# The last stage of a gated short-convolution layer: product f of its output matmul as seven smaller products

## The chip, the cores and the metric

The kernel runs on one core of a Trainium2 chip. Five engines work side by side, each through its own list of instructions in order: TensorE (PE, with its weight loads as PEld), VectorE (DVE), ScalarE (ACT), GpSimd (POOL) and SyncE (SP). SP and POOL also issue transfers (DMAs); POOL alone issues those that add to what stands at their destination. The metric is the device time of one execution in microseconds (us); before the change it is 767.92, the median of 3 runs (767.84 to 767.94).

## The reference

One layer, 1024 frames of 1024 channels, inner width 2048, all float32:

```python
u = rms_norm(x, pre_norm)                      # over the 1024 channels of a frame
z, bg, cg, v = split(u @ w_in, 4)              # w_in: 1024 x 8192
y = bg * causal_dwconv(cg * v, conv_w) * silu(z)   # 3 taps over frames, per channel
m = y @ w_out                                  # w_out: 2048 x 1024
out = x + rms_norm(m, post_norm)
```

The change concerns `m = y @ w_out` alone, and the sign with which some channels of `y` are kept.

## The kernel before, in words

**Arithmetic.** Float32 operands are split into two parts: `hi`, rounded by an ACT copy, and `lo`, the rest, by a DVE subtraction (`split_unit`). Each matmul of 128 channels x 128 frames x 512 columns is then three instructions (lo x hi, hi x lo, hi x hi; lines 929 to 931 in the last stage), with a weight load each.

**First stage** (to 607 us of the profile). `u @ w_in` in groups of three column blocks, 20 products a group (`product`, `read`), in an order written out by hand (`ORDER`). Tables say at which product of a group DVE, ACT, POOL and SP get which side work. The gated result `y` goes to memory: `y_d` holds it, `s_d` sums of its quarters, `t_d` sums of quarters of `w_out`. The sums are made by adding DMAs from POOL (`more`), each waiting for the one before where it reads its result.

**Last stage.** `y` (1024 frames x 2048 channels) and `w_out` are halved in both directions, and seven products instead of eight give the four quarters of `m`: a, b, c, e, d, f, g, in this order, each of 512 frames x 1024 channels x 512 columns. A product is 4 row tiles of 128 frames (`q`), 8 chunks of 128 channels in two halves (`h`) of four, 3 instructions each: 96 matmuls of 512 columns. a, c, d and g accumulate in the banks `po_x`, b in `po_b`, e and f in `po_v`. DVE and ACT fold them into `C11`, `C12` and `C22` (the tile `res`): `C12` holds, when f is added, all that output rows 0 to 511 need in their second half, so each of the row tiles 0 to 3 can be finished then (`norm_square` on ACT, `finish_o` on DVE, ACT and POOL, stores and the next `load_res` on SP). Rows 512 to 1023 are finished as g ends, tile by tile.

**Order around the change.** There is no scheduler: each engine's list follows the program text. The loop at the end issues for each half of a product its 48 matmuls, then four `split_unit` (operands of the product half two places later, each an ACT copy and a DVE subtraction of 128 x 1024) with two `fetch_unit` (SP transfers into the staging tiles `raw`, 6 buffers, and `u`, 18 buffers), then, after the second half, the four `combine`. For f the finishing of row tile q-1 follows the combine of tile q. g's loop runs by row tile, and within it by half: g's second half is first needed 12 matmuls after g begins.

**Signs.** `cw`, the taps of the convolution, is stored negated for channels 1024 to 2047, so that `y` of these is negative and all differences of the scheme become sums; `split_unit` turns c's operand of `w_out` back (`nc.scalar.mul(hi, src, -1.0)`).

Of the kernel before, what the change touches and what calls it, by code (L numbers as in the profile page):

```python
# [20 lines left out]
def kernel(  # L21
# [392 lines left out]


# [283 lines left out]
    nc.scalar.copy(half_of(cw, 0), half_of(pc[:, : TAPS * NC], 0))  # L699
    nc.scalar.mul(half_of(cw, 1), half_of(pc[:, : TAPS * NC], 1), -1.0)  # L700
# [111 lines left out]
    OUT = [(i, h) for i in "abcedfg" for h in (0, 1)]  # L812
    UNITS_O = [(side, i, h) for i, h in OUT for side in "uy"]
    CQ = CH // 2
    fetched, OP = [], {}

    def fetch_unit():
        n = len(fetched)
        if n >= len(UNITS_O):
            return  # L820
        side, i, h = UNITS_O[n]
        js = slice(h * CQ, (h + 1) * CQ)
        far = slice(CH + h * CQ, CH + (h + 1) * CQ)
        if side == "u":
            plain_u = {"a": wov[:, js, :HB], "b": wov[:, far, :HB], "f": wov[:, far, HB:]}
            src = plain_u[i] if i in plain_u else t_d[:, TK[i], js]
            r = []
            for q in (0, 1):
                r.append(raw.tile([P, 2, HB], F32, tag="raw", name=f"r{side}_{i}{h}{q}"))
                nc.sync.dma_start(r[q], src[:, 2 * q : 2 * q + 2])  # L830
        else:
            plain_y = {"a": y_d[:, js, :HB], "b": y_d[:, far, :HB], "g": y_d[:, far, HB:]}
            src = plain_y[i] if i in plain_y else s_d[:, SK[i], js]
            t = up.tile([P, 2, 2, HB], F32, tag="u", name=f"r{side}_{i}{h}")
            nc.sync.dma_start(t.rearrange("p a b c -> p (a b) c"), src)
            r = [t[:, 0], t[:, 1]]
        fetched.append(r)

    def split_unit(delayed=False):
        n = len(OP)  # L840
        if n >= 2 * len(UNITS_O):
            return
        side, i, h = UNITS_O[n // 2]
        q = n % 2
        t = new_u(f"o{side}_{i}{h}{q}")
        src, hi, lo = flat(fetched[n // 2][q]), flat(t[:, 0]), flat(t[:, 1])
        if (side, i) == ("u", "c"):
            nc.scalar.mul(hi, src, -1.0)
            nc.vector.scalar_tensor_tensor(lo, src, -1.0, hi.bitcast(F32), op0=ALU.mult, op1=ALU.subtract)
# [70 lines left out]
    def out_mm(i, h, q):  # L920
        which = i if i == "b" else "v" if i in "ef" else "x"
        if (which, q) not in ob:
            ob[which, q] = bank(f"po_{which}{q}")
        ps = ob[which, q]
        for k in range(CQ):
            u, y = OP["u", i, h, k // 2], OP["y", i, h, k // 2]
            hi, lo = (y[:, z, k % 2, q * P : (q + 1) * P] for z in (0, 1))
            first, last = i in "abe" and h == 0 and k == 0, h == 1 and k == CQ - 1
            nc.tensor.matmul(ps, lo, u[:, 0, k % 2], start=first, stop=False, skip_group_check=True)  # L929
# [1 line left out]
            nc.tensor.matmul(ps, hi, u[:, 0, k % 2], start=False, stop=last, skip_group_check=True)  # L931

# [60 lines left out]
    def combine(i, q):  # L993
# [8 lines left out]
        elif i == "e":  # L1002
            nc.scalar.copy(C22[:, q], v_)
        elif i == "d":
            nc.vector.tensor_add(C22[:, q], x_, C22[:, q])
            early_half(q + TH)
        elif i == "f":
            nc.vector.tensor_add(C12[:, q], v_, C12[:, q])  # L1008
            norm_square(q, 1)
# [57 lines left out]
```

## Time and profile before

| What | Value |
|---|---|
| median of the runs (lowest, highest) | 767.92 us (767.84, 767.94) |
| span of the profiled execution (first to last instruction) | 766.2 us; no other time of that execution is given |
| PE busy | 758.0 us, 99% |
| DVE, ACT, POOL busy | 485.9, 452.5, 459.7 us |
| product f, PE | 715.81 to 737.57 us |
| product g, PE | 737.57 to 759.3 us |
| mean DMA rate over the span | 152 GB/s |

The page lists busy time by engine, the chain of work that ended last (followed back from the last instruction), and groups of instructions as line, engine, operation, output<-inputs, with mean duration and what ended the idle time before them. Timeline rows begin with start and length in us. An `x2` behind a row means that two were merged. The page's busy time of PE counts pipelined matmuls that overlap; the distance between starts tells the pace. An idle engine costs nothing unless PE waits for it.

### The profile page before, as it was taken

Reading aid. Unit: us, or ns where it says so; the run is one execution under the profiler, and the core shown is the slowest. Engines: PE = TensorE matmul, PEld = TensorE weight load, DVE = VectorE, ACT = ScalarE, POOL = GpSimd, SP = SyncE. Lnnn points to the kernel's source line nnn. Section 1 sums busy time; section 2 is a strip of 40 time slices with the busy share of each in tenths; the row PEclk is TensorE's granted clock in tenths of the full one; section 3 lists DMA queues with packets and bytes.
Section 4 is the critical chain, followed back from the end, with each engine's and each line's share of the span. In section 5 each row is a group of like instructions: output and inputs, shape, how many; then the busy total and the mean of one; then the engine's idle time right before and its main releaser. Section 6 shows DMA issues by size and latency. Waiting matters only on the chain.

```text
span 766.2 us, 10006 instructions
## 1 busy us (share of the span) xinstructions
PE 758.0 (99%) x3386; PEld 627.4 (82%) x3386; DVE 485.9 (63%) x748; ACT 452.5 (59%) x881; POOL 459.7 (60%) x564
## 2 busy tenths in 40 slices
PE   9999999999999999999999999999999999999996
PEld 8888888888888888888888888888888888888885
DVE  5898776475656566656565664655566957545755
ACT  8869766557646665754666665666467735544531
POOL 0687979669676876976797796797765220000021
PEclk9999999999999999999999999999999999999999
DMA  9401335447356358165465556574545689754237
GB/s 327 142 1 64 102 97 155 133 110 191 86 154 152 94 116 213 40 183 122 134 153 128 122 151 152 124 182 98 132 97 168 205 281 373 277 189 173 79 123 261
DMA packets 103363, 116.55 MB, mean 152 GB/s; under 512 B 4696, under 2 KB 70544, under 8 KB 102288
## 3 DMA queue, kind: packets, MB, share of 16 engines
q1 hardware_dynamic: 94080, 99.13, 39.4%
q0 software_dynamic: 9216, 16.78, 14.0%
q8 instruction: 26, 0.43, 0.2%
q14 instruction: 25, 0.20, 0.1%
q10 hardware_dynamic: 16, 0.00, 0.0%
HBM read 97.02 MB, written 44.04 MB: 184 GB/s over the span
## 4 chain that ended last, share of the span: by engine, by line
PE 98%; DMA 0%; DVE 0%; ACT 0%; issue 0%; DVEq 0%
PE pX L132 8%; PE pX L134 8%; PE pX L133 8%; PE pY L132 7%; PE pY L134 7%; PE pY L133 7%; PE po_x L931 4%; PE po_x L930 4%; PE po_x L929 4%; PE pV L134 4%; PE pV L132 4%; PE pV L133 4%; PE pZ L134 2%; PE pW L134 2%; PE pW L132 2%; PE pZ L132 2%
## 5 line engine op out<-in xcount | busy, mean ns | idle before, releaser
L362 DVE TENSOR_TENSOR sn<-sn,pY 128x512 f32<-128x512 f32 x57 | 39.2, 687 | 56.4 <-PE pY L134 28.9
L969 POOL TENSOR_TENSOR res<-xr,res 128x512 f32<-128x512 f32 x4 | 6.9, 1736 | 105.4 <-DVE res L968 104.0
L338 POOL TENSOR_TENSOR g<-g,sn 128x512 f32<-128x512 f32 x29 | 40.1, 1390 | 42.2 <-ACT sn L336 35.4
L362 DVE TENSOR_TENSOR sn<-sn,pX 128x512 f32<-128x512 f32 x57 | 39.2, 688 | 33.5 <-PE pX L134 33.5
L311 POOL TENSOR_TENSOR g<-sn,g 128x512 f32<-128x512 f32 x23 | 29.9, 1298 | 47.5 <-DVE sn L360 47.5
L336 ACT ACTIVATE sn<-sn 128x512 f32<-128x512 f32 x24 | 15.2, 632 | 64.1 <-DVE sn L362 40.0
L356 ACT ACTIVATE sn<-pV 128x512 f32<-128x512 f32 x38 | 20.6, 596 | 48.0 <-PE pV L134 48.0
L320 POOL TENSOR_TENSOR g<-g,sn 128x512 f32<-128x512 f32 x20 | 28.2, 1411 | 19.2 <-DVE sn L362 18.9
L354 ACT COPY sn<-pZ 128x512 f32<-128x512 f32 x19 | 11.2, 588 | 46.6 <-PE pZ L134 46.6
L368 POOL DMA_DIRECT2D s_d<-s_d x24 | 19.8, 823 | 21.6 <-DMA s_d<-y_d 14.1
L178 POOL TENSOR_TENSOR raw<-raw 128x256 f32<-128x256 f32 x40 | 32.3, 918 | 0.0
L360 DVE TENSOR_TENSOR g<-pY,g 128x512 f32<-128x512 f32 x15 | 10.4, 692 | 30.7 <-PE pY L134 30.7
L183 POOL TENSOR_TENSOR raw<-e,raw 128x256 f32<-128x256 f32 x40 | 28.7, 739 | 1.6
L179 POOL TENSOR_TENSOR e<-raw,raw 128x512 f32<-128x512 f32 x20 | 26.2, 1312 | 1.6
L938 ACT ACTIVATE jk<-res 128x512 bf16<-128x512 f32 x12 | 7.6, 631 | 31.7 <-DVE res L1008 13.0
L132 PE MATMUL pp<-b,wn 128*128 128x512 f32 x62 | 24.6, 397 | 0.0
L133 PE MATMUL pp<-b,wn 128*128 128x512 f32 x62 | 24.3, 393 | 0.0
L134 PE MATMUL pp<-b,wn 128*128 128x512 f32 x62 | 24.2, 390 | 0.0
L301 DVE SCALAR_TENSOR_TENSOR g<-g,cw,cv 128x512 f32<-128x512 f32 x30 | 22.5, 749 | 1.7
L233 DVE TENSOR_TENSOR wE<-wE,wE 128x512 fp32r<-128x512 f32 x20 | 13.7, 686 | 14.1 <-ACT wE L232 14.0
L301 DVE SCALAR_TENSOR_TENSOR cv<-g,cw,cv 128x512 f32<-128x512 f32 x30 | 22.4, 747 | 0.0
L233 DVE TENSOR_TENSOR wC<-wC,wC 128x512 fp32r<-128x512 f32 x20 | 13.7, 687 | 11.9 <-ACT wC L228 11.9
(388 smaller groups left out, 2903.3 us busy)
## 6 DMA issues: line engine op xcount, KB each, us to landing
raw<-in_sc_w_in SPq DMA_DIRECT2D x64, 512.0 KB, 4.2
t_d<-in_sc_w_out SPq DMA_DIRECT2D x32, 256.0 KB, 4.6
s_d<-g SPq DMA_DIRECT2D x29, 256.0 KB, 2.1
s_d<-s_d POOLq DMA_DIRECT2D x24, 256.0 KB, 4.4
y_d<-g SPq DMA_DIRECT2D x23, 256.0 KB, 2.5
t_d<-in_sc_w_out POOLq DMA_DIRECT2D x16, 256.0 KB, 7.8
t_d<-t_d POOLq DMA_DIRECT2D x16, 256.0 KB, 4.8
xr<-in_x SPq DMA_DIRECT2D x8, 512.0 KB, 5.7
```

What stands on the lines that cost most here:

```text
L132: nc.tensor.matmul(ps, lo, u[:, 0, kk], start=first, stop=False, skip_group_check=True)
L133: nc.tensor.matmul(ps, hi, u[:, 1, kk], start=False, stop=False, skip_group_check=True)
L134: nc.tensor.matmul(ps, hi, u[:, 0, kk], start=False, stop=last, skip_group_check=True)
L178: 0: lambda: (add(w2[:, 0], w2[:, 0], w2[:, 1]), add(w2[:, 2], w2[:, 1], w2[:, 2])),
L183: 5: lambda: (sub(w0[:, 2], e[:, 3], w0[:, 2]), sub(w0[:, 0], e[:, 3], w0[:, 0])),
L301: nc.vector.scalar_tensor_tensor(g if j == TAPS - 1 else ps, g, tap(c, j), ps, op0=ALU.mult, op1=ALU.add)
L311: nc.gpsimd.tensor_mul(g, src, g)
L338: when([(c, "cv", h), (c, "silu", h)], (c, "z", h), {"cv": 1, "silu": 1}, lambda: nc.gpsimd.tensor_mul(cv_of(c, h), cv_of(c, h), t))
L362: nc.vector.tensor_sub(a, a, ps)
L929: nc.tensor.matmul(ps, lo, u[:, 0, k % 2], start=first, stop=False, skip_group_check=True)
L930: nc.tensor.matmul(ps, hi, u[:, 1, k % 2], start=False, stop=False, skip_group_check=True)
L931: nc.tensor.matmul(ps, hi, u[:, 0, k % 2], start=False, stop=last, skip_group_check=True)
```

## The change

Product f (`s_d["f"]` times the last quarter of `w_out`) is itself done by seven products of halved size: 256 frames (2 row tiles) x 512 channels (4 chunks) x 256 columns. They are called pieces 1 to 7 and run in the order 1, 2, 6, 5, 7, 3, 4. Each is 24 matmuls of 256 columns. What else it takes:

- Sums of quarters of f's operands, in the new memory tiles `tf_d` (from `w_out`; four plain transfers by SP at the beginning of the last group of the first stage but one, four adding ones by POOL later in it) and `sf_d` (from `s_d["f"]`; four plain and four adding ones, all by POOL, placed behind the halves of c and e).
- A small sum or difference into `C12` after each piece, on 128 x 2 x 256 numbers, by DVE. Pieces 1, 6, 7 and 4 accumulate in one bank, 5 and 3 in another, 2 has a third; a later piece of a bank waits until the earlier sum has been read from it.
- `po_v` now ends with e, which is added to `C12` too (four more DVE sums in d's time).
- Operands of a piece are two splits instead of four; both are fetched into `raw`. `refill` replaces the fixed calls of `fetch_unit`.
- Row tiles 0 and 1 are finished after piece 3, tiles 2 and 3 after piece 4.
- Negated channels are now 512 to 1535; `split_unit` turns back by product and half.

```diff
+    CQ = CH // 2
+    sf_d = dram.tile([P, 4, CQ, FC], F32, tag="sf_d", name="sf_d")
+    tf_d = dram.tile([P, 4, CQ, FC], F32, tag="tf_d", name="tf_d")
...
+    def quarter(a, i, j, k0=0, n0=0):
+        return a[:, k0 + i * CQ : k0 + (i + 1) * CQ, n0 + j * FC : n0 + (j + 1) * FC]
+    def w22(i, j):
+        return quarter(wov, i, j, CH, HB)
+    def yf(i, j):
+        return quarter(s_d[:, SK["f"]], j, i)
+    def small_t(step):
+        if step == 0:
+            for n, src in enumerate((w22(0, 0), w22(0, 0), w22(1, 1), w22(1, 0))):
+                nc.sync.dma_start(tf_d[:, n], src)
+        elif step == 1:
+            more(tf_d[:, 0], w22(0, 1))
+            more(tf_d[:, 2], w22(0, 1))
+        elif step == 2:
+            more(tf_d[:, 1], tf_d[:, 2])
+        else:
+            more(tf_d[:, 3], tf_d[:, 1])
+    def small_s(step):
+        if step == 0:
+            for n, src in enumerate((yf(1, 0), yf(0, 0), yf(1, 0), yf(0, 1))):
+                nc.gpsimd.dma_start(sf_d[:, n], src)
+        elif step == 1:
+            more(sf_d[:, 0], yf(1, 1))
+            more(sf_d[:, 2], yf(0, 0))
+        elif step == 2:
+            more(sf_d[:, 1], sf_d[:, 0])
+        else:
+            more(sf_d[:, 3], sf_d[:, 1])
...
-    nc.scalar.copy(half_of(cw, 0), half_of(pc[:, : TAPS * NC], 0))
-    nc.scalar.mul(half_of(cw, 1), half_of(pc[:, : TAPS * NC], 1), -1.0)
+    nc.scalar.copy(cw, pc[:, : TAPS * NC])
+    nc.scalar.mul(turned_chunks(cw), turned_chunks(pc[:, : TAPS * NC]), -1.0)
...
-    OUT = [(i, h) for i in "abcedfg" for h in (0, 1)]
+    FP = (1, 2, 6, 5, 7, 3, 4)
+    OUT = [(i, h) for i in "abced" for h in (0, 1)] + [("f", p) for p in FP] + [("g", 0), ("g", 1)]
...
+        if i == "f":
+            t = raw.tile([P, CQ, FC], F32, tag="raw", name=f"r{side}_f{h}")
+            nc.sync.dma_start(t, small_of(side, h))
...
+    def refill():
+        while FETCH and len(fetched) + (1 if FETCH[0][1] == "f" else 2) <= len(OP) + AHEAD:
+            fetch_unit()
...
-        if (side, i) == ("u", "c"):
+        turn = h == 6 if i == "f" else (i == "c") != (h == 1)
+        if side == "u" and turn:
...
+            if t == END - 1 and s in (2, 15, 18, 20):
+                small_t((2, 15, 18, 20).index(s))
...
+    def small_mm(p):
+        which = {1: 1, 6: 1, 7: 1, 4: 1, 2: 2, 5: 3, 3: 3}[p]
+        ...
+        for q in (0, 1):
+            o = ps[:, q * FC : (q + 1) * FC]
+            for k in range(CQ):
+                hi, lo = (y[:, z, k, q * P : (q + 1) * P] for z in (0, 1))
+                nc.tensor.matmul(o, lo, u[:, 0, k], start=p in (1, 2, 5) and q == 0 and k == 0, stop=False, skip_group_check=True)
+                nc.tensor.matmul(o, hi, u[:, 1, k], start=False, stop=False, skip_group_check=True)
+                nc.tensor.matmul(o, hi, u[:, 0, k], start=False, stop=k == CQ - 1, skip_group_check=True)
+        ps = ps.rearrange("p (a b) -> p a b", a=2)
+        for rows, cols, sign in {1: ((0, 0, 1),), 2: ((0, 0, -1),), 6: ((0, 1, -1),), 5: ((1, 1, 1),), 7: ((1, 1, 1),), 3: ((0, 1, -1),), 4: ((1, 0, -1),)}[p]:
+            c = C12[:, 2 * rows : 2 * rows + 2, cols * FC : (cols + 1) * FC]
+            if sign > 0:
+                nc.vector.tensor_add(c, ps, c)
+            else:
+                nc.vector.tensor_sub(c, c, ps)
...
         elif i == "e":
             nc.scalar.copy(C22[:, q], v_)
+            nc.vector.tensor_add(C12[:, q], v_, C12[:, q])
...
-        elif i == "f":
-            nc.vector.tensor_add(C12[:, q], v_, C12[:, q])
-            norm_square(q, 1)
...
+        if i == "f":
+            small_mm(h)
...
-        for z in range(4):
+        for z in range(2 if i == "f" else 4):
             split_unit()
-            if z % 2:
-                fetch_unit()
-        if h == 1:
+            refill()
+        if (i, h) in SMALL_S:
+            small_s(SMALL_S[i, h])
+        if i != "f" and h == 1:
             for q in range(TH):
                 combine(i, q)
-                if i == "f" and q > 0:
-                    finish_row(q - 1)
-    finish_row(TH - 1)
+        if i == "f" and h in (3, 4):
+            for q in (0, 1) if h == 3 else (2, 3):
+                norm_square(q, 1)
+                finish_row(q)
```

What this does to the order of instructions is shown at three places.

DVE before, around the end of f: the splits of g's second half (`ou_g1`, `oy_g1`), then f's first two sums (line 1008) and the finishing of row tile 0 (lines 93 to 988).

```order
L129 TENSOR_TENSOR ou_g10_6586<-ru_g10_6526,ou_g10_6586 128x1024
L129 TENSOR_TENSOR ou_g11_6589<-ru_g11_6528,ou_g11_6589 128x1024
L129 TENSOR_TENSOR oy_g10_6592<-ry_g1_6536,oy_g10_6592 128x1024
L129 TENSOR_TENSOR oy_g11_6595<-ry_g1_6536,oy_g11_6595 128x1024
L1008 TENSOR_TENSOR res_5750<-po_v0_6182,res_5750 128x512
L1008 TENSOR_TENSOR res_5750<-po_v1_6195,res_5750 128x512
L93 TENSOR_SCALAR ve_post0_6604<-so_5752,so_all_5753 128x1
L94 RECIPROCAL r0_post0_6605<-sd_post0_6602 128x1
```

DVE in the changed kernel, the same place: sum of piece 3, the first two splits of g's second half, and the beginning of row tile 0; then, after the rest of tile 0, tile 1, whose end is shown with what follows it, the sum of piece 4 and the last two splits of g.

```order
L1013 TENSOR_TENSOR res_5760<-res_5760,pf_3_6605 128x2x256
L903 SCALAR_TENSOR_TENSOR ou_g10_6699<-ru_g10_6637,ou_g10_6699 128x1024
L903 SCALAR_TENSOR_TENSOR ou_g11_6702<-ru_g11_6639,ou_g11_6702 128x1024
L96 TENSOR_SCALAR ve_post0_6708<-so_5762,so_all_5763 128x1
L97 RECIPROCAL r0_post0_6709<-sd_post0_6706 128x1
```

```order
L1050 SCALAR_TENSOR_TENSOR res_5760<-res_5760,rs_post1_6731,gpost_5756 128x512
L1070 SCALAR_TENSOR_TENSOR res_5760<-res_5760,rs_post1_6731,xr_5758 128x512
L1013 TENSOR_TENSOR res_5760<-res_5760,pf_1_6500 128x2x256
L906 TENSOR_TENSOR oy_g10_6768<-ry_g1_6672,oy_g10_6768 128x1024
L906 TENSOR_TENSOR oy_g11_6771<-ry_g1_6672,oy_g11_6771 128x1024
L96 TENSOR_SCALAR ve_post2_6777<-so_5762,so_all_5763 128x1
```

Before, the splits of g stood ahead of every sum of f and every finished row; now seven sums and the finishing of two row tiles (seven instructions each) stand ahead of the last two.

PE in the changed kernel, where d ends and piece 1 begins:

```order
L987 MATMUL po_x3_5803<-ou_d11_6322,oy_d11_6332 128x512
L988 MATMUL po_x3_5803<-ou_d11_6322,oy_d11_6332 128x512
L989 MATMUL po_x3_5803<-ou_d11_6322,oy_d11_6332 128x512
L1004 MATMUL pf_1_6500<-ou_f10_6394,oy_f10_6399 128x256
L1005 MATMUL pf_1_6500<-ou_f10_6394,oy_f10_6399 128x256
L1006 MATMUL pf_1_6500<-ou_f10_6394,oy_f10_6399 128x256
```

In all 168 instructions of 256 columns stand where 96 of 512 columns stood.

POOL in the changed kernel, from the last group but one of the first stage into the last (lines 193 to 196 make sums of `w_in` blocks, 341, 323 and 314 gate `y`, 371 issues an adding transfer):

```order
L371 DMA tf_d_80<-in_sc_w_out 128x4x256 x2
L341 TENSOR_TENSOR g_14_1_5038<-g_14_1_5038,sn_14_0_1_5375 128x512
L193 TENSOR_TENSOR e_19_5257<-e_19_5257,raw_15_3_5172 128x256
L194 TENSOR_TENSOR raw_15_3_5172<-raw_15_3_5172 128x256
L341 TENSOR_TENSOR g_14_0_5063<-g_14_0_5063,sn_14_0_0_5253 128x512
L195 TENSOR_TENSOR e_19_5257<-e_19_5257,raw_15_1_5170 128x256
L371 DMA tf_d_80<-tf_d_80 128x1024
L196 TENSOR_TENSOR raw_15_1_5170<-raw_15_1_5170 128x256
L371 DMA s_d_77<-s_d_77 128x512
L371 DMA tf_d_80<-tf_d_80 128x1024
L323 TENSOR_TENSOR g_14_0_5063<-g_14_0_5063,sn_14_1_0_5251 128x512
L314 TENSOR_TENSOR g_15_0_5314<-sn_15_3_0_5552,g_15_0_5314 128x512
```

The four transfers into `tf_d` are new in this list; the second and the third row with `tf_d` read what the one before has written.

More of the change, by code (lines that the diff above doesn't have):

```diff
@@ L810, in first_chunk, with small_of @@
             gate_y(0, 1, plain_ps[3, 1], 1, True)
-    OUT = [(i, h) for i in "abcedfg" for h in (0, 1)]
-    UNITS_O = [(side, i, h) for i, h in OUT for side in "uy"]
-    CQ = CH // 2
-    fetched, OP = [], {}
+    FP = (1, 2, 6, 5, 7, 3, 4)
+    OUT = [(i, h) for i in "abced" for h in (0, 1)] + [("f", p) for p in FP] + [("g", 0), ("g", 1)]
+    PIECES, FETCH = [], []
+    for i, h in OUT:
+        for side in "uy":
+            FETCH.append((side, i, h))
+            PIECES += [(side, i, h, q) for q in ((0,) if i == "f" else (0, 1))]
+    fetched, OP = [], {}
+    AHEAD = 4
+    def small_of(side, p):
+        if p in (5, 6, 7):
+            return (tf_d if side == "u" else sf_d)[:, p - 5]
+        if side == "u":
+            return tf_d[:, 3] if p == 4 else w22(*{1: (0, 0), 2: (1, 0), 3: (1, 1)}[p])
+        return sf_d[:, 3] if p == 3 else yf(*{1: (0, 0), 2: (0, 1), 4: (1, 1)}[p])
     def fetch_unit():
-        n = len(fetched)
-        if n >= len(UNITS_O):
+        if not FETCH:
             return
-        side, i, h = UNITS_O[n]
+        side, i, h = FETCH.pop(0)
+        if i == "f":
+            t = raw.tile([P, CQ, FC], F32, tag="raw", name=f"r{side}_f{h}")
+            nc.sync.dma_start(t, small_of(side, h))
+            fetched.append(t)
+            return
         js = slice(h * CQ, (h + 1) * CQ)
@@ L824, in fetch_unit @@
         if side == "u":
[L825 removed]
+            plain_u = {"a": wov[:, js, :HB], "b": wov[:, far, :HB]}
             src = plain_u[i] if i in plain_u else t_d[:, TK[i], js]
[L827 removed]
             for q in (0, 1):
[L829 to L830 removed]
+                r = raw.tile([P, 2, HB], F32, tag="raw", name=f"r{side}_{i}{h}{q}")
+                nc.sync.dma_start(r, src[:, 2 * q : 2 * q + 2])
+                fetched.append(r)
         else:
@@ L835, in fetch_unit @@
             nc.sync.dma_start(t.rearrange("p a b c -> p (a b) c"), src)
-            r = [t[:, 0], t[:, 1]]
-        fetched.append(r)
+            fetched.extend([t[:, 0], t[:, 1]])
+    def refill():
+        while FETCH and len(fetched) + (1 if FETCH[0][1] == "f" else 2) <= len(OP) + AHEAD:
+            fetch_unit()
     def split_unit(delayed=False):
         n = len(OP)
-        if n >= 2 * len(UNITS_O):
+        if n >= len(PIECES):
             return
-        side, i, h = UNITS_O[n // 2]
-        q = n % 2
+        side, i, h, q = PIECES[n]
         t = new_u(f"o{side}_{i}{h}{q}")
-        src, hi, lo = flat(fetched[n // 2][q]), flat(t[:, 0]), flat(t[:, 1])
-        if (side, i) == ("u", "c"):
+        src, hi, lo = flat(fetched[n]), flat(t[:, 0]), flat(t[:, 1])
+        turn = h == 6 if i == "f" else (i == "c") != (h == 1)
+        if side == "u" and turn:
             nc.scalar.mul(hi, src, -1.0)
-            nc.vector.scalar_tensor_tensor(lo, src, -1.0, hi.bitcast(F32), op0=ALU.mult, op1=ALU.subtract)
-        elif delayed:
+            low = lambda: nc.vector.scalar_tensor_tensor(lo, src, -1.0, hi.bitcast(F32), op0=ALU.mult, op1=ALU.subtract)
+        else:
             nc.scalar.copy(hi, src)
-            low_us.append(lambda: nc.vector.tensor_sub(lo, src, hi.bitcast(F32)))
+            low = lambda: nc.vector.tensor_sub(lo, src, hi.bitcast(F32))
+        if delayed:
+            low_us.append(low)
         else:
-            split(src, hi, lo)
+            low()
         OP[side, i, h, q] = t
@@ L920, in out_mm @@
     def out_mm(i, h, q):
-        which = i if i == "b" else "v" if i in "ef" else "x"
+        which = {"b": "b", "e": "v"}.get(i, "x")
         if (which, q) not in ob:
@@ L931, in out_mm @@
             nc.tensor.matmul(ps, hi, u[:, 0, k % 2], start=False, stop=last, skip_group_check=True)
+    fb = {}
+    def small_mm(p):
+        which = {1: 1, 6: 1, 7: 1, 4: 1, 2: 2, 5: 3, 3: 3}[p]
+        if which not in fb:
+            fb[which] = bank(f"pf_{which}")
+        ps = fb[which]
+        u, y = (OP[side, "f", p, 0].rearrange("p z a (b c) -> p z (a b) c", b=2) for side in "uy")
+        for q in (0, 1):
[10 more added lines that the diff above has]
+                nc.vector.tensor_add(c, ps, c)
+            else:
+                nc.vector.tensor_sub(c, c, ps)
     def halves_of(t):
@@ L1038 @@
         if q == TH - 1:
-            ob["last"] = ob["v", q][:, : HB - CUT]
+            ob["last"] = bank("last")[:, : HB - CUT]
             nc.scalar.copy(ob["last"], C22[:, q, CUT:])
```

14 lines of the change are left out of this document (8 added, 6 removed).

## The prediction

> **What bounds the kernel now.** I read the page first (busy shares, then the chain that ended last), then a table by stretch, then the timeline of the two engines that stand around product f. Times are microseconds from the start of the span.
>
> ```profile
> span 766.2 us, 10006 instructions
> PE 758.0 (99%) x3386; PEld 627.4 (82%) x3386; DVE 485.9 (63%) x748; ACT 452.5 (59%) x881; POOL 459.7 (60%) x564
> PE 98%; DMA 0%; DVE 0%; ACT 0%; issue 0%; DVEq 0%
> ```
>
> The matmul engine (PE) is the bound: 98% of the chain that ended last is its work. So a change pays only if PE issues fewer columns, and costs as soon as PE has to wait. The table by stretch (busy time and count of each engine, clock, DMA) shows a long middle piece, then products d, f and g, then the end:
>
> ```profile
> core 0: us, PE busy (x) PEld busy (x) DVE busy (x) ACT busy (x) POOL busy (x), PEclk, DMA share, GB/s
> 100.00:600.00 500.00, 500.00 (x2208) 413.85 (x2207) 303.15 (x459) 300.91 (x625) 377.24 (x477) 1.00 0.55 138
> 693.90:715.70 21.80, 21.80 (x98) 18.06 (x97) 13.52 (x17) 10.35 (x15) 0.00 (x0) 1.00 0.51 193
> 715.80:737.57 21.77, 21.77 (x97) 18.02 (x96) 14.10 (x21) 11.35 (x16) 0.49 (x1) 1.00 0.00 1
> 737.57:759.30 21.73, 21.73 (x97) 17.83 (x95) 15.74 (x45) 5.33 (x17) 6.45 (x4) 1.00 0.76 269
> 759.50:762.70 3.20, 0.00 (x0) 0.00 (x0) 2.58 (x8) 1.39 (x4) 0.45 (x1) 1.00 0.72 283
> 762.70:766.20 3.50, 0.00 (x0) 0.00 (x0) 0.20 (x1) 0.00 (x0) 0.00 (x0) 0.50 0.41 150
> ```
>
> 500 us for 2208 matmuls of 512 columns is 0.2265 us each, back to back. Product f is 96 of them (715.81 to 737.57, 21.74 us) and g another 96, so from the first matmul of f to the end of PE there are 192 x 0.2265 = 43.5 us. In f's stretch the vector engine (DVE) is busy 14.1 of 21.8 us: a cover, but no wide one. PE's end is followed by a tail of 6.9 us, which the change leaves as it is.
>
> I count against the profiled execution: its span is 766.2 us, and the median of the runs is 767.92, so 1.7 us lie outside the span. A change of the span is added to 767.9.
>
> **The matmuls.** f's 96 matmuls of 512 columns become 7 x 24 = 168 of 256 columns: 43008 columns for 49152. No matmul of 256 columns runs in this kernel, so its time is bounded from rows. One bound is the weight load, which does not shrink with the columns:
>
> ```profile
> L929 PEld LDWEIGHTS po_v<-ou_f,oy_f 128*128 128x128 f32 x32 | 6.0, 188 | 1.3
> L476 PEld LDWEIGHTS pk<-rows,xa 128*128 128x128 f32 x48 | 5.8, 191 | 0.9 <-DVE rows L636 0.8
> 11.81 0.97 PEld L476 LDWEIGHTS pk<-rows,xa 128*128 128x128 f32 x8 [0.20 <-DVE rows L636]
> ```
>
> A load shows 188 ns, but eight loads of the same size (191 ns) in the head follow each other within 0.97 us: (0.97 - 0.19)/7 = 0.111 us apart, with a matmul between them. So loads hide behind matmuls down to 0.111 us. The other bounds come from 0.2265: halved it is 0.113; if its excess over 512/256 of a column time is fixed (about 0.013), 0.120; if a load had to be waited for in full, 0.188. I take 0.1165, the middle of 0.113 and 0.120, since the head's loads at 0.111 are the nearest row. f is then 19.6 us for 21.74: PE gains 2.2 us (1.6 to 3.1; at 0.188 it loses 9.8).
>
> **What DVE has to do in that time.** Here is DVE from the end of d through f to the first finished rows, then ACT:
>
> ```profile
> 716.01 0.69 DVE L1005 TENSOR_TENSOR res<-po_x,res 128x512 f32<-128x512 f32 x1 [0.42 <-PE po_x L931]
> 717.55 0.69 DVE L953 SCALAR_TENSOR_TENSOR res<-res,gpost 128x512 f32<-128x512 f32 x1 [0.85 <-ACT jk L938]
> 718.16 0.15 DVE L955 TENSOR_SCALAR so_all<-so 128x1 f32<-128x1 f32 x1
> 718.50 2.36 DVE L129 TENSOR_TENSOR ou_g<-ru_g,ou_g 128x1024 fp32r<-128x1024 f32 x2 [0.19 <-ACT ou_g L128]
> 720.77 2.35 DVE L129 TENSOR_TENSOR oy_g<-ry_g,oy_g 128x1024 fp32r<-128x1024 f32 x2
> 723.04 2.35 DVE L129 TENSOR_TENSOR ou_g<-ru_g,ou_g 128x1024 fp32r<-128x1024 f32 x2
> 725.32 2.35 DVE L129 TENSOR_TENSOR oy_g<-ry_g,oy_g 128x1024 fp32r<-128x1024 f32 x2
> 729.62 0.69 DVE L1008 TENSOR_TENSOR res<-po_v,res 128x512 f32<-128x512 f32 x1 [1.95 <-PE po_v L931]
> 743.27 0.21 DVE L97 SCALAR_TENSOR_TENSOR nt_post<-r_post,ve_post 128x1 f32<-128x1 f32 x1
> 743.71 0.75 DVE L968 SCALAR_TENSOR_TENSOR res<-res,rs_post,gpost 128x512 f32<-128x512 f32 x1
> 744.38 0.75 DVE L988 SCALAR_TENSOR_TENSOR res<-res,rs_post,xr 128x512 f32<-128x512 f32 x1
> 745.04 0.21 DVE L93 TENSOR_SCALAR ve_post<-so,so_all 128x1 f32<-128x1 f32 x1
> 745.42 0.87 DVE L97 SCALAR_TENSOR_TENSOR nt_post<-r_post,ve_post 128x1 f32<-128x1 f32 x1
> 744.54 1.73 POOL L969 TENSOR_TENSOR res<-xr,res 128x512 f32<-128x512 f32 x1 [2.02 <-DVE res L968]
> ```
>
> Before, all eight splits of g's operands were through DVE at 727.7, ten us before g began, because the sums of f and the finished rows stood behind them in DVE's order. In the changed order the last two splits (y of g's second half, oy_g10 and oy_g11) stand behind the seven small sums and behind the finishing of output rows 0 and 1. DVE takes its instructions strictly in turn, so g's thirteenth matmul waits for all of these. Prices, as distances between starts in these rows: a sum of 512 numbers 0.61 (717.55 to 718.16), a split 1.137 (718.50 to 720.77 for two), a finished row 2.15: 0.38 (745.04 to 745.42) + 0.44 (743.27 to 743.71) + 0.67 (to 744.38) + 0.66 (to 745.04). The long L97 (0.87 for 0.21) ran while POOL worked on the row before (744.54 to 746.27); in the new order row 1 comes right behind row 0 and meets the same, 0.65.
>
> From f's first matmul: the first small sum can be read at 24 x 0.1165 + 0.20 = 3.0 (0.20 is 716.01 - 715.81) and is over at 3.6. Then come six more sums (3.66), thirteen splits up to oy_g10 (14.78), two rows (4.30), L97 (0.65) and a wait for ACT (0.15), in all 27.2; PE sees it at 27.3. DVE never waits for PE on the way: each later piece ends before DVE gets to its sum (the last at 19.6, its sum at 25). Nor does PE wait for a bank inside f: the closest is piece 4, which begins at 16.8 and writes the bank that the sum of piece 7 has read at 15.1 (3.6, eight splits, four sums). PE wants that operand at 19.57 + 12 x 0.2265 = 22.3. **It waits 5.0 us**, then runs g's other 84 matmuls, 19.0 us, and ends at 46.3 instead of 43.5: **+2.8 us**. The matmul time hardly enters: from 0.111 to 0.120 PE only waits longer or shorter for the same DVE. Without the L97 term it is +2.1; at 0.120 with it, +2.9.
>
> ACT prepares each split and must be ahead:
>
> ```profile
> 719.32 2.00 ACT L128 CAST oy_g<-ry_g 128x1024 fp32r<-128x1024 f32 x2
> 733.12 0.63 ACT L938 ACTIVATE jk<-res 128x512 bf16<-128x512 f32 x1 [2.00 <-DVE res L1008]
> 733.86 1.28 ACT L964 ACT_TABLE_LOAD   x1
> 735.16 0.29 ACT L964 ACTIVATE sd_post<-so,so_all 128x1 f32<-128x1 f32 x1
> ```
>
> Two copies take 2.00 for DVE's 2.27, so ACT leads; behind the sixth sum it squares row 0, loads the table and takes the root, 2.3 us (733.12 to 735.45), while DVE does two splits, 2.27: the 0.15.
>
> **The other edits, at nothing.** The operands of g are fetched when f's staging tiles come free, so later than before:
>
> ```profile
> ru_g<-t_d SPq DMA_DIRECT2D x4, 512.0 KB, 7.3
> ry_g<-y_d SPq DMA_DIRECT2D x2, 1024.0 KB, 6.7
> ```
>
> The first is asked for at about 5 and lands by 12.4 at the worst, DVE wants it copied at 12.4: up to 1.1 us more, which I keep for the upper end. The sums of w_out add four plain and four adding transfers in the last group but one of the first stage; the adding ones are issued by POOL, which then blocks until the one before has landed:
>
> ```profile
> L368 POOL DMA_DIRECT2D t_d<-in_sc_w_out x16 | 14.6, 1142 | 0.0
> 575.93 1.30 POOL L338 TENSOR_TENSOR g<-g,sn 128x512 f32<-128x512 f32 x1 [7.22 <-ACT sn L336]
> 590.23 1.30 POOL L311 TENSOR_TENSOR g<-sn,g 128x512 f32<-128x512 f32 x1 [6.63 <-DVE sn L360]
> 615.82 0.93 SPq L395 DMA_DIRECT2D y_d<-g  x2
> L849 DVE SCALAR_TENSOR_TENSOR ou_c<-ru_c,ou_c 128x1024 fp32r<-128x1024 f32 x4 | 4.7, 1220 | 1.5 <-ACT ou_c L848 1.5
> ```
>
> Four issues at 1.1 us (up to 4.6, were it by the number of pieces, four times as many) and two waits of a transfer's length (7.3 for ru_g above) meet idle stretches of 7.2 and 6.6 us, and what is late then (y's last chunks, stored at 615.8) is wanted at 639.7, three and a half products before f (715.81 - 3.5 x 21.74). y's sums are issued by POOL behind its last addition for f, when it has nothing else to do, and are wanted at 715. Turned signs change a copy of 48 columns and swap one kind of split for another (L849's 1220 ns, as any split that waits for ACT). e's four extra sums (2.4 us) fall into d's 21.8 us, of which DVE uses 13.5. Without these covers: some us each, counted below.
>
> **The clock.** PEclk falls to 0.50 at 762.70, 3.2 us after PE stopped. A gap of 5.0 us is longer than that. At the start PE crawled for the same reason:
>
> ```profile
> 1.44 3.32 PEld L454 LDWEIGHTS pw<-idle 128*128 128x128 f32 x15
> 4.85 1.13 PEld L454 LDWEIGHTS pw<-idle 128*128 128x128 f32 x9
> ```
>
> (3.32 - 0.33)/14 = 0.21 us a load until 4.85, 0.12 after: half speed for 3.8 us from PE's first matmul at 1.06. If the gap trips it, g loses up to 1.9 us; I take 1.6, as part of the slow time may fall into the gap. One drop in the trace does not say at which length of gap it comes, so I give it two chances in five of this case. The Trainium skill ("TensorE: Matmul & The Clock Gate", Part 1, What's actually happening) has a free-running window of 3413 ns that must be idle as a whole; by that rule a gap of 5.0 us holds one in (5.0 - 3.41)/3.41, 46% of phases, for at most 1.7 us, and the drop after 3.2 us agrees with it.
>
> **The rivals.** *Forecast:* DVE's queue makes g wait; 767.9 + 2.8 = **770.7**; chance 0.80, of which 0.32 with the clock dropping, 772.3. *The gain arrives (faster):* oy_g10 is ready in time, PE keeps its 2.2 us: 765.7. For that DVE must be 5.0 us faster between f's first sum and that split, which would be both rows out of the way; against it stands the order of the instructions; for it, that over f and g together DVE is busy only 29.8 of 43.5 us, so the work fits in sum and only its order does not. It decides at 22.3. Chance 0.07. *Loads not hidden:* at 0.13 us a matmul DVE's chain starts and is met later, f takes 21.8, the end comes about 4.2 us late, 772.1; at 0.188, f 31.6 and still some 2 us of waiting, 780. The 0.111 us loads speak against it. Chance 0.08. *POOL or the DMA rings late:* POOL's waits hold a product bank in the last group, or f's operands come late: 2 to 6 us more, 773 to 777. Chance 0.05. That the work is not reduced as said is excluded by the instruction list.
>
> **The numbers.** The measurement can tell 0.2% (1.5 us) from no change. Range 769.4 to 773.4: below, the forecast without the L97 and ACT terms and with a little less for each split (+1.5); above, the dropped clock with late operands of g (2.8 + 1.6 + 1.1). Faster 0.06 (the second case less 0.01 for a part gain), same 0.08 (that 0.01 and a low end of the forecast, 0.07), slower 0.86.
>
> **What would show it.** Right: some 168 matmuls of 256 columns 0.11 to 0.12 us apart; one gap of 4 to 6 us in PE, released by DVE's split of oy_g at about f + 27; DVE without idle time from the first small sum until then; a lower PEclk behind the gap in some executions. Wrong: matmuls of 256 columns much over 0.12, a PE gap before g or before any piece of f, or g without a gap; and if DVE shows idle time between f's sums, the sum of its work was not the limit.

## The result, and the profile after

The changed kernel takes **781.49 us** (median of 4 runs, 779.74 to 784.39) where the kernel before takes 767.93 (767.84 to 768.27): a ratio of **1.0181**, interval 1.0168 to 1.0195. It is slower by 13.6 us; the forecast was 2.8. The page of the profiled execution, head, busy shares and chain:

```profile
span 780.4 us, 10226 instructions
PE 761.1 (98%) x3458; PEld 632.6 (81%) x3458; DVE 498.4 (64%) x761; ACT 459.1 (59%) x887; POOL 471.3 (60%) x576
PE 87%; DMA 4%; POOL 3%; DVE 2%; issue 2%; ACT 1%; SPq 0%; DVEq 0%; POOLq 0%; ACTq 0%
```

The span has grown by 14.2 us. The shares of busy time hardly show it (PE 98% for 99%); the chain does: PE was 98% of it and is 87%, and DMA, POOL, "issue" and DVE have come in. So PE now waits somewhere for a chain that runs through other engines. The view of waits says where PE waited and for whom (total, times, longest):

```profile
PE pX L135 <- DVE sn L365: 6.1, 1, 6.1
PE po_x L987 <- DVE oy_g L906: 4.9, 1, 4.9
ACT oy_a L905 <- DMA ry_a<-y_d: 7.4, 1, 7.4
```

The second row is the wait that was forecast, in product g. The first is not: it lies in the first stage (bank `pX`), 120 us before product f, and the third row, ACT waiting for the first half of product a's `y`, belongs to it. Part of the table by stretch (length, busy time and count of PE, weight loads, DVE, ACT, POOL; clock, DMA share, GB/s) gives both gaps and what follows them:

```profile
603.90:610.20 6.30, 0.22 (x1) 0.00 (x0) 5.62 (x8) 3.70 (x7) 0.56 (x1) 0.92 1.07 363
610.20:616.00 5.80, 5.79 (x14) 4.53 (x15) 4.75 (x5) 3.98 (x6) 2.77 (x3) 0.50 0.69 268
616.00:727.00 111.00, 111.00 (x501) 92.28 (x500) 65.20 (x73) 52.54 (x70) 13.18 (x13) 1.00 0.83 268
747.60:752.50 4.90, 0.05 (x1) 0.00 (x0) 4.79 (x9) 2.12 (x6) 2.69 (x2) 1.00 0.69 250
752.50:756.00 3.50, 3.49 (x8) 2.78 (x9) 3.36 (x11) 0.33 (x2) 0.84 (x1) 0.51 0.71 249
```

Behind each gap the clock is at half (0.50, 0.51) for some microseconds: 14 matmuls in 5.8 us, where 3.2 us would do. From the distances between the starts of matmuls, against 0.2265 each:

| Where | us |
|---|---|
| first gap, 603.73 to 610.21 | +6.25 |
| slow matmuls behind it, to 616.0 | +2.84 |
| f's 168 matmuls of 256 columns, 20.16 for 21.74 | -1.58 |
| second gap, 747.26 to 752.51 | +5.02 |
| slow matmuls behind it | +1.73 |
| sum (the span grew by 14.2) | +14.26 |

Product f begins at 724.59 for 715.81: 8.8 us are lost before it, and 5.4 from there on. Two items outside the table cancel: up to the first gap PE runs 0.26 us earlier than before, and the tail behind its last matmul is 0.24 us longer.

**Where the first gap comes from.** The chain that ended last, followed through it (start, length, what):

```profile
569.93 6.61 issue
576.54 6.88 DMA tf_d<-in_sc_w_out
...
583.78 6.72 DMA tf_d<-tf_d
...
590.84 0.81 POOL tf_d L371
591.65 1.35 POOL g L323
593.01 0.34 SPq L397
593.40 0.42 SPq L398
593.92 9.46 DMA ry_a<-y_d
603.40 1.06 ACT oy_a L905
604.48 1.23 DVE oy_a L906
```

POOL issues the adding transfers of `tf_d` (the new sums of w_out) and each holds POOL until the one before has landed. Behind the fourth stands the gating of a chunk of `g` (L323), behind that, on SP, the stores of this chunk (L397, L398), and behind the stores, in SP's order, the fetch of `ry_a`, the first half of `y` for product a. The same places in the timeline of the kernel before (its lines 320, 394, 395, 835 and 851 are 323, 397, 398, 886 and 905 in the change), on POOL, SP and ACT, and then, of its transfers issued from 584.4 to 584.7, size and us from issue to landing:

```profile
582.02 1.59 POOL L320 TENSOR_TENSOR g<-g,sn 128x512 f32<-128x512 f32 x1
590.23 1.30 POOL L311 TENSOR_TENSOR g<-sn,g 128x512 f32<-128x512 f32 x1 [6.63 <-DVE sn L360]
583.63 0.34 SPq L394 DMA_DIRECT2D s_d<-g  x1
584.02 0.42 SPq L395 DMA_DIRECT2D y_d<-g  x1
584.53 0.40 SPq L835 DMA_DIRECT2D ry_a<-y_d  x1
595.74 1.05 ACT L851 CAST oy_a<-ry_a 128x1024 fp32r<-128x1024 f32 x1
```

```profile
ry_a<-y_d SPq DMA_DIRECT2D x1, 1024.0 KB, 7.2
```

In the change the gating is this row of POOL's timeline:

```profile
591.38 1.60 POOL L323 TENSOR_TENSOR g<-g,sn 128x512 f32<-128x512 f32 x1
```

The gating stood at 582.02 and now stands at 591.38; the fetch of `ry_a` at 584.53, now at 593.92: 9.4 us later. It landed 7.2 us later, at 591.7, and ACT took it at 595.74: 4 us to spare. Now landing takes 9.5 us, too, and ACT waits until 603.40 with all that stands behind this copy in its list, DVE waits behind ACT, and PE for the banks that DVE should have read. POOL's idle 6.63 us of before lies *behind* the gating, not ahead of it: the new waits did fall into idle time in sum, but they pushed the gating to the end of it.

**The second gap** is the forecast one. DVE from the long instruction of row 1 to the splits that g waits for (last row, two of them):

```profile
747.75 0.85 DVE L100 SCALAR_TENSOR_TENSOR nt_post<-r_post,ve_post 128x1 f32<-128x1 f32 x1
...
750.76 2.83 DVE L906 TENSOR_TENSOR oy_g<-ry_g,oy_g 128x1024 fp32r<-128x1024 f32 x2
```

### The profile page after: what moved, and what is told of

Same layout as the page of the kernel before. It is cut to its first block, busy times and chain, and to the rows that moved or that the text cites. A ratio compares the mean times of both kernels' runs of the same rounds, so it can differ in the third digit from the quotient of the medians.

```text
span 780.4 us, 10226 instructions
## 1 busy us (share of the span) xinstructions
PE 761.1 (98%) x3458; PEld 632.6 (81%) x3458; DVE 498.4 (64%) x761; ACT 459.1 (59%) x887; POOL 471.3 (60%) x576
## 4 chain that ended last, share of the span: by engine, by line
PE 87%; DMA 4%; POOL 3%; DVE 2%; issue 2%; ACT 1%; SPq 0%; DVEq 0%; POOLq 0%; ACTq 0%
PE pX L135 7%; PE pX L136 7%; PE pX L137 7%; PE pY L136 6%; PE pY L135 6%; PE pY L137 6%; PE po_x L987 4%; PE po_x L988 4%; PE po_x L989 4%; PE pV L136 3%; PE pV L135 3%; PE pV L137 3%; PE pW L136 2%; PE pZ L136 2%; PE pW L137 2%; PE pZ L137 2%
## 5 line engine op out<-in xcount | busy, mean ns | idle before, releaser
L323 POOL TENSOR_TENSOR g<-g,sn 128x512 f32<-128x512 f32 x20 | 28.3, 1414 | 19.2 <-DVE sn L365 18.9
L357 ACT COPY sn<-pZ 128x512 f32<-128x512 f32 x19 | 11.2, 589 | 46.7 <-PE pZ L137 46.7
L135 PE MATMUL pX<-b,wJ 128*128 128x512 f32 x40 | 16.3, 408 | 6.1 <-DVE sn L365 6.1
```

The lines of the kernel that those rows point to most:

```text
L135: nc.tensor.matmul(ps, lo, u[:, 0, kk], start=first, stop=False, skip_group_check=True)
```

## The experiments

Each time stands beside runs of the kernel before on the same chip (768.04 to 768.15). Theory from here on: two separate gaps. The first is SP's order behind POOL's late gating, the second DVE's order. Rivals: the first gap is due to POOL's waits or to the bytes of the new transfers themselves; the second goes elsewhere when it is undone; smaller matmuls cost more than counted.

### The first gap

**e_sp_front**: only the fetch of `ry_a` moved ahead, in front of the late chunk's stores on SP; POOL's work and all bytes stay.

```diff
             product(t, i)
+            if t == END and s == 1:
+                fetch_unit()
...
-            if t == END - 1 and s == 14 or t == END and s in (2, 8, 13, 15, 17):
+            if t == END - 1 and s == 14 or t == END and s in (8, 13, 15, 17):
```

> The changed kernel with one transfer moved: SP issues the fetch of the first product's y one product earlier, ahead of chunk 14's two stores instead of behind them. POOL's waits, the additions and all bytes stay. My theory (SP's order carries POOL's lateness to PE): the gap before the last stage goes, 772.7 (771 to 775, the second half's operands are still late by some 9 us). If POOL's lateness reaches PE in another way, or the rings are crowded, the gap stays: 779 to 782.

Measured: 774.95 (773.83 to 777.17), ratio 1.0100 (1.0084 to 1.0117); 6.5 us below the change. SP and POOL in the timeline of this kernel, then the stretch in which the gap was:

```profile
581.42 0.37 SPq L886 DMA_DIRECT2D ry_a<-y_d  x1
594.00 0.33 SPq L397 DMA_DIRECT2D s_d<-g  x1
591.86 0.81 POOL L371 DMA_DIRECT2D tf_d<-tf_d  x1 [4.60 <-DMA tf_d<-tf_d]
```

```profile
596.00:612.00 16.00, 16.00 (x72) 13.27 (x71) 14.39 (x16) 9.96 (x15) 5.42 (x6) 1.00 1.03 323
```

POOL waits as long as in the change (4.60) and the late chunk is stored as late (594.00), but the fetch is out at 581.42, and PE is busy throughout: 72 matmuls in 16.0 us at full clock. The DMA engines are as full as in the gap of the change (1.03 for 1.07). So this gap comes neither from POOL's waits in themselves nor from the bytes; it comes from what stood behind them on SP. The second gap is still there, 5.39 us with 1.70 of slow matmuls in the profiled run, the shortest of four; the four lie 3.3 us apart, and what the longer ones lost is not seen. The median is 2 us above the expected 772.7.

**e_spread**: the other way round; SP's order stays, and the sums are spread over two groups so that POOL is less late at that chunk (`small_add(n)` issues the n-th adding transfer alone).

```diff
-            if t == END - 1 and s in (2, 15, 18, 20):
-                small_t((2, 15, 18, 20).index(s))
+            if t == END - 2 and s == 2:
+                small_t(0)
+            if t == END - 1 and s in (2, 7, 12, 17):
+                small_add((2, 7, 12, 17).index(s))
```

> The changed kernel with the additions of w_out's sums moved: the four plain transfers one group earlier, the four adding ones one by one at the products 2, 7, 12 and 17 of the last group but one instead of 15, 15, 18 and 20. My theory: the 6.3 us gap of PE before the last stage came because POOL stood waiting for these additions with the gating of chunk 14 behind it, behind that its store on SP, and behind that store, in SP's order, the fetch of the first product's y. Then the gap and the slow clock after it go (6.3 + 0.4 + 11 x 0.2 = 8.8 us): 781.5 becomes 772.7 (771 to 774.5), with the gap in g still there. Rival: the extra bytes as such crowd the DMA rings and make that fetch late; they are still moved, so 779 to 782.

Measured: 774.84 (774.63 to 775.35), ratio 1.0089 (1.0074 to 1.0104). POOL still waits for its transfers, 5.6 and 1.2 us for the last two, but the gating is at 587.04, and the fetch of `ry_a` goes out at 589.55: 5.0 us later than before, 4.4 earlier than in the change. The first gap is gone too, but for two delays of 0.1 to 0.2 us; ACT still waits 1.8 us for `ry_a` (7.4 in the change), so this cover is just used up. The second gap is 5.24 us here with 2.82 of slow matmuls, one step of slow clock more than in the profile of e_sp_front.

**e_before_sums**: the kernel before, with the sums of w_out as the change makes them, and nothing else (nobody uses them).

```diff
+    tf_d = dram.tile([P, 4, CQ, FC], F32, tag="tf_d", name="tf_d")
...
+            if t == END - 1 and s in (2, 15, 18, 20):
+                small_t((2, 15, 18, 20).index(s))
```

> The kernel before, with only the sums of w_out of the change added (four plain and four adding transfers at the changed kernel's places); nothing reads them. My theory: this alone opens the gap of some 6 us before the last stage and the slow clock behind it: 767.9 + 8.8 = 776.7 (774 to 779). If the gap needs other parts of the change: 767.9 to 769.

Measured: 775.32 (772.46 to 776.57), ratio 1.0090 (1.0069 to 1.0111): +7.3 us from an edit that the prediction had priced at nothing. Its waits and the stretch of the gap:

```profile
PE pX L134 <- DVE sn L364: 6.6, 1, 6.6
ACT oy_a L872 <- DMA ry_a<-y_d: 7.5, 1, 7.5
```

```profile
603.80:610.50 6.70, 0.12 (x1) 0.00 (x0) 5.59 (x8) 4.10 (x6) 0.62 (x2) 0.80 1.06 363
```

The same gap at the same place, with no product of 256 columns in the kernel. Its four runs lie 4.1 us apart: the shortest (span 770.7) has a mean clock of 0.998, as the kernel before, the longest (774.8, the profiled one) 0.994. What the clock takes behind the gap thus differs from run to run.

### The second gap

**e_rows_last**: output rows 0 to 3 finished behind all splits of g's operands.

```diff
-        if i == "f" and h in (3, 4):
-            for q in (0, 1) if h == 3 else (2, 3):
-                norm_square(q, 1)
-                finish_row(q)
...
+    for q in range(TH):
+        norm_square(q, 1)
+        finish_row(q)
```

> The changed kernel with the finishing of output rows 0 to 3 moved behind the last splits of g on every engine. My theory: DVE's queue made g wait; the gap of 5.0 us and the slow clock after it (in the profile 0.3 + 6 x 0.2 + 0.2) go: 781.5 - 6.7 = 774.8 (773.5 to 776.5). What could take some of it back is the chain of two row buffers at the end, which begins some 4 us later: up to 2 us. Rival: DVE is short in sum over f and g, so that the waiting only moves to the end: 778 to 781.

Measured: 777.5 (777.04 to 780.66), ratio 1.0132 (1.0111 to 1.0153), 4 us below the change. The gap in g is gone (0.1 us is left of it), which shows that DVE's queue made it. But PE's last matmul is 12.6 us before the end of the span, where it was 7.4: a new tail, which the expectation had allowed for with up to 2 us. It is taken up below.

The 4 us are not the price of the gap in g alone, because the first gap differs as well, although no instruction ahead of it was edited. In this profile PE loses 1.52 us at 593 and 3.00 at 606, 4.5 in all, with no slow clock behind either. The late gating now runs on POOL (590.50 to 593.34) beside a DVE split that took 1.22 us in the profile of the change:

```profile
590.88 3.55 DVE L906 TENSOR_TENSOR ou_a<-ru_a,ou_a 128x1024 fp32r<-128x1024 f32 x1
```

PE waits for DVE's next read of a bank. The profile of e_row1_late has the same (3.74 us for this split, then gaps of 1.72 and 3.41). So POOL's lateness can reach PE by this second way too, and the first gap costs different amounts in different runs: 4.5 to 9.1 us in these profiles.

**e_row1_late**: only row 1 moved behind the splits.

```diff
-            for q in (0, 1) if h == 3 else (2, 3):
+            for q in (0,) if h == 3 else (1, 2, 3):
```

> The changed kernel with row tile 0 finished after piece 3 as it is, but row tile 1 only behind the last splits of g. The gap in g should shrink by one row, 2.8 us with its long small operation, from 5.0 to 2.2 us. If the clock drops only for a gap longer than about 3.4 us, it stays up in g and the time is 781.5 - 2.8 - 1.7 = 777.0; if a gap of 2.2 us trips it too, 778.7. If rows are not the cause, no change: 781.5.

Measured: 778.31 (776.44 to 778.58), ratio 1.0126 (1.0109 to 1.0143). The wait in g falls from 5.02 to 3.14 us, that is by 1.9 for a row priced at 2.15 and a delay of 0.65; ACT and the fetches of g (DVE waits 0.9 us for ACT there) take a part back.

**e_both**: e_spread and e_rows_last together. 

> Both moves together, f still as seven pieces. If the two gaps are all that the change cost beside f's gain, 781.5 - 8.8 - 6.7 = 766.0 (765 to 767.5), faster than the kernel before by f's 1.6 us and little else, and the runs agree within 0.5 us again, as no gap is long enough to trip the clock. If the sums' transfers or the end of the rows cost something of their own, 768 to 771.

Measured: 772.21 (771.42 to 772.38), ratio 1.0052 (1.0037 to 1.0067). PE ends at 758.2, 0.9 us *before* that of the kernel before (759.1), with one wait left (0.36 us); and still the kernel is 4 us slower. The chain that ended last shows the rest:

```profile
743.85 0.34 SPq L1032
744.24 3.65 DMA xr<-in_x
748.02 1.80 POOL res L1057
749.84 0.33 SPq L1032
750.26 4.49 DMA xr<-in_x
754.85 0.75 DVE gx L1074
...
756.72 5.22 DMA xr<-in_x
762.03 0.75 DVE gx L1074
```

There are two buffers for rows of x (`xr`). Each row is fetched when the row two before it is done with, and lands 3.7 to 5.2 us later. With all rows finished in g's time, these fetches stand one behind the other until the end.

### The matmuls

**e_before_256**: the kernel before, with f's matmuls each as two of 256 columns: 192 for 96, the same product.

```diff
+            for c in (slice(0, FC), slice(FC, HB)) if i == "f" else (slice(0, HB),):
+                nc.tensor.matmul(ps[:, c], lo, u[:, 0, k % 2, c], start=first, stop=False, skip_group_check=True)
...
```

> The kernel before, with each of product f's matmuls done as two of 256 columns (192 for 96), nothing else changed. At 0.120 us each, as in the changed kernel's trace, f takes 192 x 0.120 = 23.0 us for 21.7: 769.2 (768.9 to 769.6). At 0.113, half of a wide one, no change: 767.9. This is the price of the narrow matmul without the scheme's saving.

Measured: 769.43 (768.96 to 769.66), ratio 1.0018 (1.0009 to 1.0028): +1.4 us, so a matmul of 256 columns takes (21.74 + 1.4)/192 = 0.1205 us. In the change their starts are 0.120 apart. The loads stay hidden; what does not halve is a fixed part of about 0.013.

### The tail, and what is left of the gain

**e_both_xr3**: e_both with three row buffers. 

> Edit: as e_both, with three row buffers of x instead of two (loads of output rows 0, 1 and 2 ahead of f). Theory: in e_both the tail of 11.4 us behind PE's last matmul was set by these buffers, since each of rows 2 to 7 could be fetched only when the row two before it was through DVE and POOL. With three the tail returns to the 7.1 us of before; PE ends at 758.2 as in e_both; span 765.3, time 767.4 (766.5 to 768.5), so no loss against before. Rival: the tail is the work itself, four more rows on DVE and POOL in g's time; then it stays over 10 us and the time over 771.

```diff
-    xr = p2.tile([P, 2, D], F32, tag="xr", name="xr")
+    xr = p2.tile([P, 3, D], F32, tag="xr", name="xr")
...
-        if t + 2 < NT:
-            load_res(t + 2)
+        if t + 3 < NT:
+            load_res(t + 3)
```

Measured: 768.05 (766.96 to 769.16), ratio 0.9999 (0.9990 to 1.0008): the loss is gone, as expected. DVE waits 0.6 us for rows of x (4.1 in e_both).

**e_best**: also the sum of piece 4 behind g's last splits on DVE. 

> Edit: as e_both_xr3, and DVE's sum of piece 4 behind the last two splits of g's operands instead of ahead of them. Theory: the one gap left, 0.58 us at the twelfth matmul of g, is DVE's queue again: 0.61 us earlier on DVE, and the gap is closed to 0.1 or less; 766.9 (766.0 to 768.0). Rival: that gap is the fetch of g's y (ACT waited 1.2 us for it) and stays; time as e_both_xr3.

```diff
+        if i == "f" and h == FP[-1]:
+            kept = small_product(h)
...
+    small_sum(FP[-1], kept)
     for q in range(TH):
```

Measured: 768.06 (766.76 to 768.81), ratio 1.0000 (0.9991 to 1.0009). In the profile PE has no wait left and ends at 756.9, 2.2 us earlier than before the change, yet the time does not move: a miss. DVE waits 0.9 us for rows of x, so PE's earlier end mostly lengthens the tail. The profiled run (766.88) is one of the shortest of eleven; what the longer ones lose is not seen.

**e_front_xr3**: e_sp_front with the rows last and three buffers, the sums bunched as in the change. 

> Edit: the sums of w_out stay as in the change, bunched on POOL in the last group but one; the fetch of y for the first product one product earlier in SP's order (as e_sp_front), output rows 0 to 3 finished behind all splits, three row buffers. Theory: POOL's waits cost only through what stands behind them on SP, so the time is that of e_both_xr3 within 1 us, 767.4 (766.5 to 768.5). Rival: POOL's late chunk also holds something else that e_sp_front's longer time hid; then 1 to 3 us more than e_both_xr3, with a gap in PE before 640.

Measured: 767.85 (766.88 to 769.29), ratio 0.9999 (0.9990 to 1.0008). POOL's bunched waits cost nothing once the fetch stands in front of them: the first theory holds in this kernel too.

**e_before_xr3**: the kernel before with three buffers. 

> Edit: the kernel before with three row buffers instead of two, nothing else. Theory: before, rows 0 to 3 are finished early and the buffers were no limit; 767.9 (within 0.5 of before). Rival: part of the tail of 7.1 us was theirs too; 766 to 767, and what three buffers give to the other kernels is not to be put down to the change.

Measured: 767.91 (767.51 to 768.58), ratio 0.9998 (0.9989 to 1.0007): nothing. The third buffer only repairs what moving the rows does.

**e_rows_held**: e_best without reuse of row buffers; rows 2 to 7 go to the six staging tiles that g's splits leave free.

```diff
+        if t > 1:
+            kept_rows[t] = raw.tile([P, 2, HB], F32, tag="raw", name=f"x_{t}")
+        nc.sync.dma_start(row_of(t), xf[t * P : (t + 1) * P, :].rearrange("p (e d) -> p e d", e=NE))
...
+    for t in range(2, NT):
+        load_res(t)
     small_sum(FP[-1], kept)
```

> Edit: as e_best, but no row of x waits for a buffer: rows 0 and 1 in the two row buffers, rows 2 to 7 in the six staging tiles of 128 x 1024 that g's last splits leave free, fetched ahead of the last small sum. Theory: in e_best DVE still waited 0.9 us for rows of x near the end and its last chain began 1.9 us behind PE's last matmul, where before it was 1.1; without it the tail is 7.1 to 7.4 us behind a PE that ends at 756.9, span 764.2, and the time 0.5 to 0.9 us below e_best and the kernel before: 767.3 (766.6 to 768.0), ratio 0.999. Rival: six rows fetched at once collide with the stores of the finished rows and with g's y; then a gap in g or the old tail, 768 to 770.

Measured: **766.92** (766.10 to 767.93) against 768.07, ratio **0.9985** (0.9976 to 0.9994): 1.1 us faster than the kernel before. The head of its page and the end of its chain:

```profile
span 764.8 us, 10236 instructions
```

```profile
757.63 0.24 PE po_x L995
...
758.61 0.70 DVE po_x L1073
```

No fetch stands in the chain; it ends with PE's last product and DVE's, as before the change. PE's last matmul is at 757.5 for 759.1, which is the 1.6 us that f's matmuls save (1.58); with a tail of 7.4 us for 7.1, 1.1 to 1.4 of it reach the time.

## Why the prediction was wrong

By the steps of the prediction:

- **The matmuls**: 0.1165 was taken, 0.120 came (f and e_before_256), the bound of its own with the excess fixed. The gain is 1.58 us, not 2.2. By the prediction's argument a longer f only shortens the wait in g; it did not, as DVE came 0.6 later too (next point).
- **What DVE has to do in that time**: right. PE waits 5.0 us for `oy_g` 12 matmuls into g (forecast 5.0; measured 5.02), behind the finishing of rows 0 and 1, with the long L100 (0.85, forecast 0.87; e_rows_last removes the wait). The split came at f + 27.9 for 27.3, mostly because the last two splits took 2.83 us while POOL worked (2.35 in the rows of the price). That the wait is 5.0 to the tenth is luck: f's longer matmuls and DVE's lateness, 0.6 us each, cancel in it.
- **The clock**: it dropped behind this gap, which had been given two chances in five of the main case, and cost 1.73 us (1.6 was taken). With this, the stretch from f on is 5.4 us longer; the forecast with the drop was 4.4; the missing 1.0 is DVE's later split (0.6), the tail (7.4 for 7.1 us) and the clock (0.1). The drop at the end of the kernel before was read too kindly: 3.2 us is less than 3.41, so taken strictly that row speaks against a window that must be idle as a whole, not for it.
- **"The other edits, at nothing"** is the step that failed, in its sentence on the sums of w_out: that the two waits "meet idle stretches of 7.2 and 6.6 us", and that what is late then is "y's last chunks, stored at 615.8" and "wanted at 639.7". Three things were wrong in it. The second idle stretch lay behind the gating of a chunk on POOL, not ahead of it, so a wait put ahead of the gating delayed it by up to the whole stretch (582.02 to 591.38). The second adding transfer waited too, 6.6 us, beside the third and fourth (1.2 and 4.7). And the work behind the gating was followed only to its stores: in SP's order the fetch of `ry_a` stood next, wanted 11.2 us after its issue and landing in 7.2 (9.5 in the change). In the profiled run this is 9.1 us (6.25 and 2.84), two thirds of the loss; e_before_sums has it alone (+7.3), e_sp_front removes it by SP's order alone.
- **The rivals**: the mechanism had a place ("POOL or the DMA rings late: POOL's waits hold a product bank"), with a chance of 0.05 and 2 to 6 us. The chance came from the step above, which had found cover for it. The other rivals did not occur: loads stayed hidden, and the gain did not arrive.
- **What it would be worth**: the case "the gain arrives" was priced at 2.2 us with PE as the only bound. With every wait removed (e_rows_held) it is 1.1 us, 1.58 less what the longer tail takes.

## What to carry to other kernels

Idle time on an engine covers a new wait only if it stands in front of the next instruction on that engine that somebody wants; so follow a late instruction through every queue behind it, the transfer queues too, down to the first thing that has less slack than the delay, and price it by that slack. When work is moved behind a deadline, look for what it now meets there: the finishing of rows cost 5 us in front of g's operands, and 4 us of tail behind them until the row buffers were made enough. A single late fetch at the end of a stage stops ACT, DVE and PE in turn, as each takes its list in order, and a gap of this size is paid for a second time by the clock.

## What the runs showed of the hardware

**The clock behind a gap.** In each trace the changes of the granted clock lie on a grid of 3.413 us (in the change from 604.16 us at full clock, 177 steps, to 6.83 at half, 2 steps). With stretches cut on this grid, the change and then e_row1_late read:

```profile
602.38:605.79 3.41, 1.74 (x8) 1.12 (x6) 1.31 (x2) 2.33 (x5) 0.82 (x1) 1.00 1.06 409
605.79:609.20 3.41, 0.00 (x0) 0.00 (x0) 3.31 (x5) 1.86 (x2) 0.00 (x0) 1.00 1.08 323
609.20:612.62 3.42, 2.41 (x6) 1.93 (x7) 3.42 (x5) 0.63 (x1) 1.28 (x1) 0.50 1.05 407
612.62:616.03 3.41, 3.41 (x10) 2.63 (x9) 2.36 (x3) 3.40 (x5) 2.05 (x2) 0.50 0.43 168
```

```profile
745.72:749.13 3.41, 0.43 (x2) 0.39 (x3) 3.41 (x5) 2.94 (x9) 1.66 (x1) 1.00 0.42 157
749.13:752.55 3.42, 3.42 (x10) 2.65 (x9) 3.28 (x12) 0.30 (x1) 1.20 (x1) 0.50 0.48 155
```

A step with no matmul is followed by half clock, and so is one with 0.43 us of them (13%), in a gap of only 3.14 us; a step that is half full (1.74 of 3.41) is not. At half clock, the step that still holds 1.0 us of the gap (2.41 busy of 3.42) is followed by another at half, a full one by full clock. So a gap costs one or two steps, by its place on the grid: beside the gap itself 1.5 to 1.7 us with one, 2.0 to 2.8 with two. The Trainium skill ("TensorE: Matmul & The Clock Gate", Part 1, What's actually happening) has the free-running window of 3413 ns, and the traces agree; that it must be idle as a whole, as the prediction took it, they do not bear out. A gap of 3.14 us was enough, one of 3.00 in e_rows_last, which left both steps that it touched half full (1.72 and 2.27 of 3.41), was not, and gaps of 5 to 7 us were followed by half clock in every profile that had one.

**POOL's adding transfers.** The second adding transfer into `tf_d` writes another quarter than the first and reads nothing of it, and yet POOL issued it only about 0.3 us after the first had landed. In the changed kernel, the transfer issued from 567 to 570 (size, us to landing), and the next one in POOL's timeline:

```profile
tf_d<-in_sc_w_out POOLq DMA_DIRECT2D x1, 512.0 KB, 7.8
```

```profile
576.54 1.25 POOL L371 DMA_DIRECT2D tf_d<-in_sc_w_out  x1 [6.61 <-issue]
```

Issued at 568.39, landed 7.8 later at 576.2, the next one out at 576.54. In e_spread it is 559.08 + 7.1 = 566.2 and 566.47, in e_before_sums 568.92 + 8.7 = 577.6 and 577.97. The profile names no releaser, and what holds POOL there stays open; no run took it apart. It is no rule of adding transfers: earlier in the same kernel two into `t_d`, of 256 KB each, went out together and landed 6.9 us later in the median,

```profile
515.12 1.95 POOL L371 DMA_DIRECT2D t_d<-in_sc_w_out  x2
```

and a plain transfer of POOL's into `sf_d` (653.36) was held too, 7.97 us. For the time it does not matter once the fetch stands in front: e_front_xr3 has the same transfers and is no slower than e_both_xr3.
